# Weight tiles of another pitch and other fills beside two attentions, in a one-layer hybrid trunk

## The chip, the cores and the metric

The kernel runs on one core of a Trainium2 chip. The metric is the time of one execution in microseconds (us) on the device. A profiled execution has a time of its own, and its span, from the first to the last instruction, is a little shorter. Line numbers (L140) are those of the kernel before.

## The reference, cut to what matters

One residual layer over 1024 tokens of width 1024, all in float32:

```python
h = rmsnorm(x, norm1_g);  u = h @ w_in            # columns: mixers A, B, C, D and four gates
y_a = b_gate * conv3(c_gate * xa)                 # A: short gated convolution
y_b = stick_breaking_attention(q_b, k_b, v_b)     # B: 4 heads of 64
y_c = mamba2_mixer(u_c, ...)                      # C: conv4 + silu, dt = softplus, chunked scan, z gate
y_d = moba_attention(q_d, k_d, v_d)               # D: softmax attention over key blocks
merged = sum(sigmoid(u_g[i]) * (y_i @ w_branch[i]) for i in range(4))
x = x + merged @ w_o
g, up = split(rmsnorm(x, norm2_g) @ w_gate_up);  x = x + (silu(g) * up) @ w_down
return rmsnorm(x, final_g)
```

Both convolutions are causal: at the left edge they see zeros.

## The kernel before, in words

Every float32 matrix product is made of three matmuls (`mm3`, L137 to 142): each operand is split into a high part and a rest (`split`, L144: ScalarE writes the high part, VectorE subtracts), and high x high, high x rest and rest x high are added up in PSUM. A matmul has a stationary operand of 128 x 128 (the weights, loaded by LDWEIGHTS, "PEld" in the profile) and streams a moving operand of 512 columns.

SBUF tiles come from one pool with tags. Tag "w" has 8 buffers, each 1040 columns of four bytes wide, 4160 bytes a partition (`tw`, `PW`), of which nearly all tiles use 1024 columns. Tag "b" has 14 buffers of 4096 bytes, "t" has 6 of 8192. A tile waits for the release of the buffer that it takes over. The two sizes above 1024 columns are the weights of z and dt (`wz`, two tiles of 4 x 260 columns) and the inputs of the convolutions, which keep three (`craw`) or two (`cx`) columns of zeros at the left edge, set by GpSimd (L486, L624), and read shifted ranges behind them.

The stages follow each other:

- Head: x is normed, transposed and split into hT (`h0h`, `h0l`, `h1h`, `h1l`), eight token tiles in turn; `z_dt` (L243) makes z and dt of each tile, in an order written out by hand (`in_order`).
- `ssd` (L480): mixer C, with convolution, and beside it the projections of the first attention and `short_conv(0)`.
- Four attentions (`attend`, L386): two of softmax (mixer D), two of stick-breaking (mixer B, `stick_rows`: two sigmoids on ScalarE, a scan and a product on VectorE). Each goes through 8 units (2 heads x 4 query blocks of 256) with 1, 2, 3 and 4 steps, 20 steps in all. A step transposes two blocks of weights (`trp`, L403), splits them (`pt`) and multiplies the `pt` of the step before with v (`o`, L413).
- Beside an attention runs other work: `Fill` (L196) holds a list of generators and is called twice a step; `per_step` is how many turns of a generator a step brings. One turn is one `mm3` of 512 columns. `block` (L289) loads one weight tile and takes 16 turns; `qkv` and `short_conv` have three blocks each, 48 turns; `projected` has 32. `take` has no turns: it loads a branch's y and its projection weights (`w_branch`) and splits them. `fill.finish()` at an attention's end runs what is left.
- Branch products of A and B (`pr`, L823 on), with the sums of hT that the next stage needs (`sums_of_h`, on GpSimd and VectorE).
- Gates (`combine`, L766): 16 groups, each with seven products `prod` of 12 matmuls, from four token blocks by a scheme with sums (`four`). w[1], w[2] (operand `h0`), w[6] (`t2`) and w[7] (`t3`) are split into "w" tiles, w[5], w[3] (`h1`) and w[4] (`t4`) into "b" tiles.
- Output projection (moving operands in "w"), second norm and early products (`early`), FFN up (22 groups like the gates; `g` in place of `h`; the first 12 have two products less), and the last product (`product`, L1079), whose operands are in turn two "w" pairs (`hi`, `lo`) and three "t" pairs (`dhl`) of five.

The order on each engine is made once, before the run, from the whole program: mostly as written, with work drawn forward where an engine would stand idle.

The lines that order the fills are these:

```python
fill.gens += [qkv(B0, 1, sts[3])]
attend(sts[2], 0, stick_rows, 1, 2.4)
fill.gens += [take(2, c_), projected(2, c_), take(3, d_), short_conv(1, nc.gpsimd), projected(3, d_)]
attend(sts[3], 1, stick_rows, 1, 4.6)
```

Of the kernel before, what the change touches and what calls it, by code (L numbers as in the profile page):

```python
# [31 lines left out]
F32 = mybir.dt.float32  # L32
F32R = mybir.dt.float32r
# [6 lines left out]
P = 128  # L40
# [6 lines left out]
NEG = -1e30  # L47
PW = 1040
A0, B0, X0, D0 = 0, 6, 12, 16
# [3 lines left out]
def tile_hybrid_trunk(  # L53
# [31 lines left out]

    def tw(name, dt=F32):
        return mn.tile([P, PW], dt, tag="w", name=name, bufs=NB["w"])

    def big(name, tag="b", dt=F32):
        if tag == "w":  # L90
            return tw(name, dt)[:, :1024]
        return mn.tile([P, 1024], dt, tag=tag, name=name, bufs=NB[tag])
# [36 lines left out]

    def load_w(src, n=1024):  # L130
        raw = tw("wraw")
        nc.sync.dma_start(raw[:, :n], src)
        hi, lo = tw("whi", F32R), tw("wlo", F32R)
        split(hi[:, :n], lo[:, :n], raw[:, :n])
        return hi, lo
# [8 lines left out]
    def split(hi, lo, v):  # L144
        nc.scalar.copy(hi, v)  # L145
        nc.vector.tensor_sub(lo, v, hi.bitcast(F32))  # L146
# [49 lines left out]
    class Fill:  # L196
# [14 lines left out]

        def finish(self):
            self(1e9)

# [6 lines left out]
    dt = cp.tile([P, 8, 4], F32, name="dt")  # L221
    g1 = tw("g_sb")[:, :D]
    c2 = halves(big("c2a")) + halves(big("c2b"))
# [19 lines left out]
    def z_dt(t):  # L243
        o = psum("mm", "mmz")[:, :260]
        h = hT[t // 4]
        tl = slice((t % 4) * P, (t % 4 + 1) * P)
        for k in range(NK):
            if k == 4:
                yield
            w = wz[k // 4]  # L250
            c = slice((k % 4) * 260, (k % 4 + 1) * 260)
            mm3(o, (h[0][:, k, tl], h[1][:, k, tl]), (w[0][:, c], w[1][:, c]), k == 0, k == NK - 1)
        sg = c2[t % 4]
        nc.scalar.activation(sg[:, :256], o[:, :256], AF.Sigmoid)
        nc.vector.tensor_mul(sg[:, 256:], o[:, :256], sg[:, :256])
        nc.vector.tensor_add(dt[:, t, :], o[:, 256:260], dtb)
        nc.sync.dma_start(zdr[:, t, :], sg[:, 256:])

    load_x(0)
    nc.scalar.dma_start(g1, norm1_g.partition_broadcast(P))  # L260
    load_x(1)
    with in_order():
        norm1_stat(0)
        norm1_scale(0)
        norm1_stat(1)
        wz = [load_w(wzdt[0], 1040)]
        load_x(2)
        norm1_turn(0)
        norm1_scale(1)
        norm1_stat(2)  # L270
        wz.append(load_w(wzdt[1], 1040))
        for t in range(3, 8):
# [112 lines left out]

    def attend(st, p, rows, br, per_step):  # L386
        vv = st[3]
# [30 lines left out]
        for n, (j, cc) in enumerate(units):  # L418
# [18 lines left out]
            nc.gpsimd.dma_start(ydr[br][r, p, cc * 256:(cc + 1) * 256], yo[r])  # L437
        fill.finish()

# [40 lines left out]
    def ssd(per_chunk):  # L480
# [3 lines left out]
        for m in range(4):  # L484
            raw = tw("craw")
            nc.gpsimd.memset(raw[:, 0:3], 0.0)  # L486

            def put(half, t, o):
                nc.scalar.copy(raw[:, 3 + t.start:3 + t.stop], o)

            for _ in block(X0 + m, put):
                pass
            if m == 0:
                steps()
            acc = s8[0][:, m] if m < 2 else fm[:, m - 2]
            nc.vector.tensor_scalar(acc, raw[:, 3:3 + S], wc[:, m, 3:4], bc[:, m:m + 1],
                                    op0=ALU.mult, op1=ALU.add)
            for j in range(3):
                nc.vector.scalar_tensor_tensor(acc, raw[:, j:j + S], wc[:, m, j:j + 1], acc,
                                               op0=ALU.mult, op1=ALU.add)  # L500
            nc.scalar.activation(raw[:, :S], acc, AF.Sigmoid)
            nc.vector.tensor_mul(acc, acc, raw[:, :S])
            if m < 3:
# [118 lines left out]
    def short_conv(m, q=nc.sync):  # L622
        xa, cx = tw("xa"), tw("cx")
        nc.gpsimd.memset(cx[:, 0:2], 0.0)  # L624

        def put_x(_, t, o):
            nc.scalar.copy(xa[:, t], o)

        def put_c(_, t, o):
            nc.vector.tensor_mul(cx[:, 2 + t.start:2 + t.stop], o, xa[:, t])  # L630
            nc.vector.tensor_scalar_mul(xa[:, t], cx[:, 2 + t.start:2 + t.stop], wa[:, m, 2:3])
            for j in range(2):
                nc.vector.scalar_tensor_tensor(xa[:, t], cx[:, j + t.start:j + t.stop], wa[:, m, j:j + 1],
                                               xa[:, t], op0=ALU.mult, op1=ALU.add)

        def put_b(_, t, o):
            nc.vector.tensor_mul(xa[:, t], o, xa[:, t])

        yield from block(A0 + m, put_x)
        yield from block(A0 + 4 + m, put_c)  # L640
        yield from block(A0 + 2 + m, put_b)
        q.dma_start(ydr[0][:, m, :], xa[:, :S])

# [14 lines left out]
    def take(i, got):  # L658

        y = [[big(v, dt=F32R) for v in ("yhi", "ylo")] for _ in range(2)]  # L660
        w = [t8([2, 1024], "wbr") for _ in range(2)]
        w = [[v[:, 0], v[:, 1]] for v in w]
        for k in range(2):
# [28 lines left out]
    s8[0] = t8([2, S], "s8", F32)  # L692
    fill.gens += [qkv(B0, 1, sts[3])]
    attend(sts[2], 0, stick_rows, 1, 2.4)
    c_, d_ = [], []
    fill.gens += [take(2, c_), projected(2, c_), take(3, d_), short_conv(1, nc.gpsimd), projected(3, d_)]
    attend(sts[3], 1, stick_rows, 1, 4.6)
    pps.close()
# [546 lines left out]
```

## Time and profile before

| | |
|---|---|
| time, median of 3 runs | 1629.99 us (1629.48 to 1630.47) |
| the profiled execution | 1629.49 us, span 1627.8 us |
| TensorE matmuls (PE) | 1574.7 us busy, 7385 of them |
| weight loads (PEld) | 1285.0 us busy |
| VectorE (DVE) | 1175.8 us busy |
| ScalarE (ACT) | 660.5 us busy |
| GpSimd (POOL) | 187.5 us busy |

Busy times of different engines overlap. Matmuls are pipelined, and the end of each is modelled: a row of 0.39 us can be followed by the next one 0.23 us after its start, so the distance from start to start is what a matmul costs in a run of them. The granted clock (PEclk) is the share of TensorE's full clock that the chip granted.

### The profile page before, as it was taken

What the parts mean: (1) busy time and instruction counts of PE and PEld (TensorE: products, weight loads), DVE (VectorE), ACT (ScalarE), POOL (GpSimd) and SP (SyncE); (2) the same over time, 40 slices, a digit from 0 to 9 for tenths busy, and PEclk for the clock granted to TensorE, in tenths of its full rate; (3) what the DMA queues carried; (4) which work ended last, traced back from release to release, by engine and by line L of the source; (5) the groups of instructions that cost most, each with busy time, mean ns of one, the idle gap of its engine ahead of it and who ended that gap; (6) DMA issues with size and microseconds to landing.
All of it is one profiled execution on the core that took longest, in us unless ns stands there. A gap on an engine that the chain in (4) does not pass through costs nothing.

```text
span 1627.8 us, 20199 instructions
## 1 busy us (share of the span) xinstructions
PE 1574.7 (97%) x7385; PEld 1285.0 (79%) x7385; DVE 1175.8 (72%) x1725; ACT 660.5 (41%) x1072; POOL 187.5 (12%) x311
## 2 busy tenths in 40 slices
PE   6999999988999899999999999899999999999997
PEld 6888778776888688888887887688778888888885
DVE  5575687787674878777876547689999877656566
ACT  5343356565645633333333435321223322354343
POOL 1011020211205200000000011011001000010310
PEclk9999999999999999999999999999999999999999
DMA  4221211112316624343347545456764334897612
GB/s 172 69 93 63 74 35 35 42 40 70 135 53 214 241 85 155 111 147 104 130 129 257 208 149 180 157 216 231 262 241 187 149 149 149 309 407 255 189 49 104
DMA packets 88036, 245.97 MB, mean 151 GB/s; under 512 B 10400, under 2 KB 15552, under 8 KB 87936
## 3 DMA queue, kind: packets, MB, share of 16 engines
q1 hardware_dynamic: 69792, 181.49, 32.9%
q0 software_dynamic: 17712, 61.61, 9.5%
q10 hardware_dynamic: 432, 1.57, 0.3%
q8 instruction: 58, 0.95, 0.2%
q14 instruction: 42, 0.34, 0.1%
HBM read 172.00 MB, written 72.63 MB: 150 GB/s over the span
## 4 chain that ended last, share of the span: by engine, by line
PE 82%; DVE 10%; ACT 3%; issue 2%; DMA 2%; POOL 0%; SPq 0%; DVEq 0%; ACTq 0%; POOLq 0%
PE acc L156 13%; PE pp L140 12%; PE pp L142 12%; PE pp L141 12%; PE mm L140 4%; PE mm L142 4%; PE mm L141 4%; PE pp L156 4%; PE o L413 3%; PE acc L141 2%; PE acc L142 2%; PE trp L403 2%; PE acc L140 2%; DVE s L383 1%; DVE lo L146 1%
## 5 line engine op out<-in xcount | busy, mean ns | idle before, releaser
L145 ACT CAST hi<-s 128x1024 fp32r<-128x1024 f32 x76 | 77.2, 1049 | 179.8 <-DVE s L718 166.4
L156 PE MATMUL acc<-dhl 128*128 128x512 f32 x540 | 125.6, 390 | 0.0
L156 PEld LDWEIGHTS acc<-dhl 128*128 128x128 f32 x540 | 101.4, 188 | 21.3
L146 DVE TENSOR_TENSOR lo<-raw,hi 128x1024 fp32r<-128x1024 f32 x62 | 78.0, 1266 | 39.5 <-ACT hi L145 39.5
L146 DVE TENSOR_TENSOR lo<-s,hi 128x1024 fp32r<-128x1024 f32 x76 | 90.4, 1223 | 11.7 <-ACT hi L145 11.7
L785 ACT ACTIVATE g<-g 128x512 f32<-128x512 f32 x38 | 24.1, 633 | 154.2 <-DVE g L784 126.9
L145 ACT CAST hi<-raw 128x1024 fp32r<-128x1024 f32 x62 | 64.8, 1049 | 41.3 <-DMA raw<-in_wgu_dram 18.8
L146 DVE TENSOR_TENSOR dhl<-dr,dhl 128x1024 fp32r<-128x1024 f32 x45 | 58.4, 1311 | 30.7 <-ACT dhl L156 27.6
L146 DVE TENSOR_TENSOR pt<-trp,pt 128x512 fp32r<-128x512 f32 x80 | 54.5, 685 | 27.7 <-ACT pt L145 26.8
L140 PE MATMUL mm<-h0h,whi 128*128 128x512 f32 x176 | 73.0, 415 | 0.0
L140 PE MATMUL mm<-h1h,whi 128*128 128x512 f32 x176 | 72.9, 414 | 0.0
L156 ACT CAST dhl<-dr 128x1024 fp32r<-128x1024 f32 x45 | 47.1, 1052 | 58.5 <-PE acc L156 24.5
L141 PE MATMUL mm<-h0l,whi 128*128 128x512 f32 x176 | 70.3, 399 | 0.0
L142 PE MATMUL mm<-h0h,wlo 128*128 128x512 f32 x176 | 70.1, 398 | 0.0
L142 PE MATMUL mm<-h1h,wlo 128*128 128x512 f32 x176 | 70.0, 397 | 0.0
L141 PE MATMUL mm<-h1l,whi 128*128 128x512 f32 x176 | 69.9, 397 | 0.0
L413 PE MATMUL o<-pt,vv 128*128 128x256 f32 x320 | 60.6, 292 | 8.3 <-DVE pt L146 7.8
L142 PE MATMUL pp<-g1h,lo 128*128 128x512 f32 x176 | 68.6, 390 | 0.0
L140 PE MATMUL pp<-g1h,hi 128*128 128x512 f32 x176 | 68.5, 389 | 0.0
L141 PE MATMUL pp<-g1l,hi 128*128 128x512 f32 x176 | 68.5, 389 | 0.0
L413 PEld LDWEIGHTS o<-pt,vv 128*128 128x128 f32 x320 | 50.1, 190 | 22.6 <-DVE pt L146 12.7
L145 ACT CAST pt<-trp 128x512 fp32r<-128x512 f32 x80 | 47.2, 598 | 46.6 <-PE trp L403 43.7
(380 smaller groups left out, 4553.6 us busy)
## 6 DMA issues: line engine op xcount, KB each, us to landing
raw<-in_wgu_dram SPq DMA_DIRECT2D x56, 512.0 KB, 4.4
dr<-ffd SPq DMA_DIRECT2D x77, 256.0 KB, 4.5
raw<-in_wgate_dram SPq DMA_DIRECT2D x32, 512.0 KB, 5.3
raw<-prd SPq DMA_DIRECT2D x32, 512.0 KB, 4.2
wraw<-in_wmix_dram SPq DMA_DIRECT2D x22, 512.0 KB, 3.6
raw<-in_wd_dram SPq DMA_DIRECT2D x22, 512.0 KB, 4.3
wdd<-fs POOLq DMA_DIRECT2D x22, 512.0 KB, 3.5
ffd<-fs POOLq DMA_DIRECT2D x22, 512.0 KB, 4.0
```

The source lines that it names most:

```text
L140: nc.tensor.matmul(o, ah, bh, start=start, stop=False)
L141: nc.tensor.matmul(o, ah, bl, start=False, stop=False)
L142: nc.tensor.matmul(o, al, bh, start=False, stop=stop)
L145: nc.scalar.copy(hi, v)
L146: nc.vector.tensor_sub(lo, v, hi.bitcast(F32))
L156: setattr(e, n, lambda *a, _f=f, **k: tc.keep_in_program_order(_f(*a, **k)))
L383: nc.vector.tensor_tensor_scan(r, r, r, 1.0, ALU.mult, ALU.bypass)
L403: nc.tensor.transpose(tr[:, s * 256 + e * P:s * 256 + (e + 1) * P], pq[e][:, (s0 + s) * P:(s0 + s + 1) * P], identf)
L413: nc.tensor.matmul(o, vv[:, s0 + s, j, :], pt[:, i, s * 256:(s + 1) * 256], start=s0 + s + i == 0, stop=s0 + s + i == ns)
L785: nc.scalar.activation(g0[:, 512:], g0[:, 512:], act)
```

## The change

- Every "w" tile is 1024 columns, 4096 bytes; there are still 8. `g_sb`, the gain of the first norm, moves to a "b" tile.
- The weights of z and dt, 8 x 260 columns, are loaded into three tiles of 780, 780 and 520 columns, four loads in place of two, with the raw values in "w" and the two parts in "b" (`load_z`).
- The convolutions keep no zeros: the first term covers all columns and each shifted term only the columns that it reaches. The memsets go.
- The second short convolution stands behind the projections of the fourth attention, beside the third; the third has 3.6 turns a step instead of 2.4 and leaves one generator unfinished (`finish(left=1)`); the fourth has the rest of the convolution and both projections at 3.4 turns instead of 4.6.
- The weights of the second projection (`take(3)`) are split into "w" tiles instead of "t" tiles.

```diff
-PW = 1040
-    def tw(name, dt=F32):
-        return mn.tile([P, PW], dt, tag="w", name=name, bufs=NB["w"])
     def big(name, tag="b", dt=F32):
-        if tag == "w":
-            return tw(name, dt)[:, :1024]
         return mn.tile([P, 1024], dt, tag=tag, name=name, bufs=NB[tag])
...
-        def finish(self):
-            self(1e9)
+        def finish(self, left=0):
+            while len(self.gens) > left:
+                if next(self.gens[0], "end") == "end":
+                    self.gens.pop(0)
...
-    g1 = tw("g_sb")[:, :D]
+    g1 = big("g_sb")
...
-            w = wz[k // 4]
-            c = slice((k % 4) * 260, (k % 4 + 1) * 260)
+            w = wz[k // 3]
+            c = slice((k % 3) * 260, (k % 3 + 1) * 260)
...
+    def load_z(*src):
+
+        raw, hi, lo = big("zraw", "w"), big("zhi", dt=F32R), big("zlo", dt=F32R)
+        n = 0
+        for v in src:
+            nc.sync.dma_start(raw[:, n:n + v.shape[-1]], v)
+            n += v.shape[-1]
+        split(hi[:, :n], lo[:, :n], raw[:, :n])
+        return hi, lo
...
-        wz = [load_w(wzdt[0], 1040)]
+        wz = [load_z(wzdt[0][:, :780])]
...
-        wz.append(load_w(wzdt[1], 1040))
+        wz.append(load_z(wzdt[0][:, 780:], wzdt[1][:, :520]))
+        wz.append(load_z(wzdt[1][:, 520:]))
...
-        fill.finish()
+        fill.finish(left)
...
-            raw = tw("craw")
-            nc.gpsimd.memset(raw[:, 0:3], 0.0)
+            raw = big("craw", "w")
 
             def put(half, t, o):
-                nc.scalar.copy(raw[:, 3 + t.start:3 + t.stop], o)
+                nc.scalar.copy(raw[:, t], o)
...
-            nc.vector.tensor_scalar(acc, raw[:, 3:3 + S], wc[:, m, 3:4], bc[:, m:m + 1],
-                                    op0=ALU.mult, op1=ALU.add)
+            nc.vector.tensor_scalar(acc, raw, wc[:, m, 3:4], bc[:, m:m + 1], op0=ALU.mult, op1=ALU.add)
             for j in range(3):
-                nc.vector.scalar_tensor_tensor(acc, raw[:, j:j + S], wc[:, m, j:j + 1], acc,
+                nc.vector.scalar_tensor_tensor(acc[:, 3 - j:], raw[:, :S - 3 + j], wc[:, m, j:j + 1], acc[:, 3 - j:],
                                                op0=ALU.mult, op1=ALU.add)
...
-        xa, cx = tw("xa"), tw("cx")
-        nc.gpsimd.memset(cx[:, 0:2], 0.0)
+        xa, cx = big("xa", "w"), big("cx", "w")
...
-        w = [t8([2, 1024], "wbr") for _ in range(2)]
-        w = [[v[:, 0], v[:, 1]] for v in w]
+        if i == 2:
+            w = [t8([2, 1024], "wbr") for _ in range(2)]
+            w = [[v[:, 0], v[:, 1]] for v in w]
+        else:
+            w = [[big(v, "w", F32R) for v in ("whi", "wlo")] for _ in range(2)]
...
-    fill.gens += [qkv(B0, 1, sts[3])]
-    attend(sts[2], 0, stick_rows, 1, 2.4)
+    fill.gens += [qkv(B0, 1, sts[3]), short_conv(1, nc.gpsimd)]
+    attend(sts[2], 0, stick_rows, 1, 3.6, 1)
     c_, d_ = [], []
-    fill.gens += [take(2, c_), projected(2, c_), take(3, d_), short_conv(1, nc.gpsimd), projected(3, d_)]
-    attend(sts[3], 1, stick_rows, 1, 4.6)
+    fill.gens += [take(2, c_), projected(2, c_), take(3, d_), projected(3, d_)]
+    attend(sts[3], 1, stick_rows, 1, 3.4)
```

The convolution inside `short_conv` is changed in the same way as the one in `ssd`.

## Rows read from the trace of the kernel before

**Rows 1.** The page, busy time of the engines, share of the span, instructions

```profile
PE 1574.7 (97%) x7385; PEld 1285.0 (79%) x7385; DVE 1175.8 (72%) x1725; ACT 660.5 (41%) x1072; POOL 187.5 (12%) x311
```

**Rows 2.** Busy time by stretch: third and fourth attention, branch products, gates, FFN

```profile
321.00:396.00 75.00, 67.70 (x386) 53.55 (x384) 58.16 (x74) 43.49 (x92) 13.48 (x26) 1.00 0.18 57
396.00:508.00 112.00, 109.01 (x556) 89.32 (x555) 71.23 (x85) 64.28 (x124) 22.75 (x47) 0.98 0.35 121
508.00:560.00 52.00, 46.43 (x199) 37.16 (x198) 44.51 (x48) 31.15 (x53) 25.35 (x27) 0.99 0.56 206
560.00:869.00 309.00, 309.00 (x1342) 252.88 (x1341) 235.54 (x287) 103.41 (x132) 1.60 (x3) 1.00 0.38 131
...
1025.00:1410.00 385.00, 378.21 (x1631) 307.11 (x1630) 317.77 (x430) 102.97 (x135) 35.75 (x67) 0.99 0.56 199
```

**Rows 3.** Matmuls in order of time, first rows of products in two gate groups

```profile
598.92 0.40 PE L140 MATMUL pp<-h0h,hi 128*128 128x512 f32 x1
...
607.27 0.39 PE L140 MATMUL pp<-t3h,hi 128*128 128x512 f32 x1
...
609.99 0.39 PE L140 MATMUL pp<-h1h,hi 128*128 128x512 f32 x1
...
612.71 0.39 PE L140 MATMUL pp<-t4h,a 128*128 128x512 f32 x1
...
626.53 0.39 PE L140 MATMUL pp<-t3h,hi 128*128 128x512 f32 x1
...
629.32 0.39 PE L140 MATMUL pp<-h1h,hi 128*128 128x512 f32 x1
...
637.48 0.40 PE L140 MATMUL pp<-h0h,hi 128*128 128x512 f32 x1
```

**Rows 4.** Groups by line: count, busy us, mean ns, idle before

```profile
L140 PE MATMUL mm<-h0h,whi 128*128 128x512 f32 x176 | 73.0, 415 | 0.0
...
L140 PE MATMUL pp<-t2h,hi 128*128 128x512 f32 x152 | 61.2, 403 | 4.2 <-ACT hi L145 4.1
...
L140 PE MATMUL pp<-h0h,hi 128*128 128x512 f32 x128 | 51.4, 402 | 3.9 <-ACT pr L835 3.9
...
L156 PE MATMUL pp<-g0h,hi 128*128 128x512 f32 x96 | 38.5, 402 | 0.0
...
L140 PE MATMUL pp<-g0h,hi 128*128 128x512 f32 x80 | 31.6, 396 | 0.0
```

**Rows 5.** Matmuls of the last product, first row of two runs

```profile
1446.14 0.39 PE L156 MATMUL acc<-hi 128*128 128x512 f32 x1
...
1451.69 0.39 PE L156 MATMUL acc<-dhl 128*128 128x512 f32 x1
```

**Rows 6.** Waits of TensorE, 321 to 396 us, then 405.8 to 508: us, times, longest

```profile
PE o L413 <- DVE pt L146: 6.9, 6, 1.8
...
PE o L413 <- DVE pt L146: 0.3, 1, 0.3
```

**Rows 7.** Busy time by stretch at the fourth attention's start

```profile
397.00:402.40 5.40, 3.15 (x16) 1.73 (x14) 5.26 (x11) 4.61 (x10) 0.20 (x1) 1.00 0.48 155
402.40:405.80 3.40, 3.32 (x13) 3.13 (x14) 3.40 (x6) 2.23 (x6) 0.12 (x1) 0.51 0.00 0
```

**Rows 8.** Instructions in order of time in the head, SyncE's queue and TensorE

```profile
6.29 0.33 SPq L132 DMA_DIRECT2D wraw<-in_wzdt_dram  x1
...
14.12 1.07 PE L156 MATMUL trn<-identf,xn 128*128 128x128 f32 x8
16.24 0.38 PE L156 MATMUL mmz<-whi,h0h 128*128 128x260 f32 x1 [1.06 <-ACT whi L156]
...
20.00 1.90 PE L156 MATMUL trn<-identf,xn 128*128 128x128 f32 x8 [0.90 <-DVE ss L156]
```

**Rows 9.** A group by line, from 40 to 330 us

```profile
L486 POOL MEMSET craw<- 128x3 f32 x3 | 0.9, 304 | 23.1 <-DVE wlo L146 17.6 <-PE mmz L156 5.6
```

## The prediction before the change was run

> **What bounds the kernel now.** I read the page first, then the busy time by stage, then single matmuls in order of time, then the waits of TensorE. The page shows TensorE busy for 97% of the span and VectorE for 72% [rows 1]. So a gain can come only from TensorE's few idle places or from matmuls that follow each other faster. By stage, TensorE stands idle for 7.3 us of the third attention (75.0 less 67.7) and 3.0 us of the fourth (112.0 less 109.0), for 5.6 us of the two branch products after it, and for nothing in the gate stage [rows 2]. In the gate stage the distance from matmul to matmul is then the whole time.
>
> That distance has two sizes, which the group means hide. The product of w[7] with t3 has 12 matmuls. From its first row to the first row of the next product it takes 609.99 - 607.27 = 2.72 us in one gate group and 629.32 - 626.53 = 2.79 us in the next [rows 3]: 227 against 232 ns each. Line, operand t3 and shapes are the same, and TensorE waits for nothing. What differs is which of the eight "w" buffers holds the weights. 4160 is 4096 + 64, so the eight buffers start at eight different offsets from a multiple of 4096; "b" and "t" tiles have pitches of 4096 and 8192 and all start alike. I read the two sizes as a price of the start address of the weights, paid in most "w" tiles and in no other.
>
> **The change, part by part.** The sum is made against the profiled execution, 1629.5 us (span 1627.8).
>
> *Pitch 4096.* Two consecutive gate groups, 168 matmuls in 14 products, run from 598.92 to 637.48 [rows 3]: 38.56 us. At 2.72 a product they would take 38.08. So the 96 matmuls of the pair that take weights from "w" lose 0.48 us together, 5.0 ns each. Eight pairs: 3.8 us. The FFN takes "w" weights for t2 and t3 in all 22 groups (528 matmuls), for the first two products in ten groups (3 x 80) and in the early products (3 x 96) [rows 4]: 1056 x 5.0 ns = 5.3 us. In the last product 24 matmuls with both operands in "w" tiles take 1451.69 - 1446.14 = 5.55 us [rows 5], 231 ns. There are 384 of them, and 384 of the output projection that only stream from "w". At 4.6 ns each and three quarters of the buffers: 2.6 us. The 1056 matmuls of the input projection (six groups of 176) [rows 4] would give 5.3 us. They run beside attention, whose waits would take back some, so I count half, 2.6. The 192 branch products stand in a stage with VectorE busy 44.5 of 52 us [rows 2]; I count nothing. Together 14.3. Some of the FFN's saving goes into its own waits (TensorE idle 6.8 of 385 us there [rows 2]). I take **12.5 us**. Bounds: 9 (gates and FFN alone) and 15 (all counted).
>
> Here the Trainium skill speaks against the change. "TensorE: Matmul & The Clock Gate", section "Step-by-step: what each phase is for", says that the next weights come in through a read port of their own while a matmul streams, and that their load time goes by the number of columns; an address does not appear in it. By that rule this term is 0 and the sum below is -5.5. Rows 3 show one instruction at two speeds, which that rule leaves unexplained, so I follow the rows.
>
> *The fill rates.* One turn of the fill is three matmuls, 3 x 0.23 = 0.70 us. The third attention has 20 steps at 2.4 turns, 48 in all, exactly what its projection has: 1.7 us of cover a step. It is too little: TensorE waits 6.9 us in six places for pt, which VectorE splits after a scan [rows 6]. The fourth has 4.6 turns a step and waits 0.3 us after its start [rows 6]. At its start, with the fill used up, 5.4 us hold 3.15 us of TensorE work, and in the 3.4 us behind them the granted clock is 0.51, the lower of two levels, 1.2 GHz [rows 7]: 2.25 idle and 1.7 lost to the clock, 3.9 us.
>
> After the change the third attention has 72 turns: 48 of the projection and 24 of the short convolution. The other 24 are left, and the fourth has 68 paced turns of 24 + 64. So 20 turns, 14 us, run unpaced at the end, as before (92 of 112). The start of the fourth then always has turns ready: most of the 3.9 us goes, I count 3.5. The steady waits are 6.9 at 2.4 turns and 0.3 at 4.6; at 3.6 and 3.4 a straight line gives 3.3 and 3.9, no gain. A queue's waits fall faster than a line at first, so I take 2.0 and 2.2: 3.0 us gained. Together **6.5**. Bounds: 0 (straight line, and VectorE late at the start anyway) and 11 (all waits gone). VectorE pays for the moved 24 turns: one and a half blocks of weights split and half a convolution, some 6 us more in the third and less in the fourth. It was busy 58 of 75 us there and would be busy 64 of some 87; that fits, but little room is left.
>
> *Weights of z and dt.* Two loads of 1040 columns become four loads into tiles of 780, 780 and 520. The first z product then needs the second tile already at k = 3, and the next transposes stand behind it on TensorE in written order. Now the second load is issued at 6.29 us behind six of x, the transposes of the next token tile run at 14.12 and the second half of z waits until 16.24 [rows 8]. After: k = 3 stalls from 13.6 to about 16.3, the transposes follow it, and the two smaller splits cost one more fixed part on ScalarE and VectorE. The chain to the next row of transposes at 20.00 waits 0.9 us for its own scale [rows 8], which is the slack. I take **1.0 us lost**; bounds 0.5 gained (the first load is a quarter smaller) and 4 lost (two late splits and a spell at the lower clock, which at the fourth attention's start cost 1.7).
>
> *Convolutions.* The memsets of the left edge (0.3 us on GpSimd [rows 9]) go, and the shifted operations are one to three columns shorter. No product waits for those memsets: nothing either way; if one did, its 0.3 us.
>
> *Projection tiles.* The weights of the second projection stand in "w" rather than "t". Four of the eight "w" tiles are then held until its end. Branch 1's weights can use them only from there on, 20 us before they are needed at 531; the wait for the first gate weights, 3.9 us [rows 4], stays, since it follows VectorE's sums. Counted at nothing, hidden behind branch 0's products; the rival below prices it when that cover fails.
>
> Sum: -12.5 - 6.5 + 1.0 = -18.0, so 1611.5 us for the profiled execution, and with the median of before half a microsecond higher, **1612**.
>
> **The rivals.** *The fill only moves the waits.* VectorE is near its limit in the third attention, and what TensorE gains there it loses in the fourth at 3.4 turns. For it: the straight line above. Against: the start of the fourth is a gap that a left-over generator fills by construction. Time: 1629.5 - 12.5 + 1.0 + 0.5 = 1618.5.
>
> *The pitch does nothing.* The two speeds would come from something else that alternates with the groups, such as writes of the next weights. Against: the product behind the fast one takes its weights from "b" tiles, which are written in the same way, and needs 612.71 - 609.99 = 2.72 us [rows 3]. Time: 1630.0 - 6.5 + 1.0 = 1624.5. "SBUF — State Buffer", section on Door 1, gives lines of 16 bytes as the grain of full bandwidth; 4160 and 4096 are both multiples of 16, which agrees with this rival. No row here shows lines.
>
> *Slower: "w" tiles run out in the fourth attention.* The convolution holds two and its last block three; take(2) needs raw tiles, take(3) four more and raw tiles. If the loads and splits of both takes get their tiles only when the convolution is over and then queue one behind another, the projections are not ready. Each step without cover loses what VectorE is short of: its 58 us over 20 steps are 2.9 a step, against (67.7 - 48 x 0.70) / 20 = 1.7 of TensorE's own work [rows 2], so 1.2 us, and up to 1.6 with the latency. With 13 steps bare that is 21, plus 6 for a load and split in the open: 1612 + 27 = 1639. It decides when the first projection matmul comes later than the middle of the fourth attention; if only the second projection is late, half: about 1626 to 1628, no change. Against: the six tiles left beside the convolution suffice for a block's three and the raw tiles of a take, and 24 turns at 3.4 end a third of the way in.
>
> **How the numbers follow.** My forecast 66%, moved waits 14%, no pitch effect 8%, tiles short 7%, half short 5%. A measurement of this kernel tells about 0.2%, 3.3 us, from no change. The first three are faster by more than that: 88%; half short is the same, 5%; tiles short is slower, 7%. The bounds of the terms (9 to 15, 0 to 11, +0.5 to -4) put the likeliest case between 1604 and 1622; the range goes on to 1625 to take in the third case.
>
> **What would show it.** Right: every product of 12 matmuls at 2.72 us in the gate stage, and the last product's runs of 24 at 5.44; six waits for pt in the third attention shrunk to two or three; no spell at the lower clock near the fourth's start; first matmul of the input projection within 1 us of 47.8. Wrong: products at two speeds still; projection matmuls missing in the fourth attention's first half; the wait of 3.9 us at the gates longer. What would upset the sum most is another order of the instructions around the attentions, since the order is made anew from the whole program.

## The result, and the profile after the change

The changed kernel takes 1615.64 us (median; 1612.7 to 1616.85 in four runs) against 1629.74 us for the kernel before on the same chip (1627.42 to 1630.47). The ratio is 0.9913, with a 95% interval of 0.9896 to 0.993: 14 us faster. The forecast was 1612.0, its range 1604 to 1625. The profiled execution of the changed kernel took 1616.02 us, with a span of 1614.3. Line numbers below are those of the changed kernel: L134 to L136 are `mm3`, L139 and L140 `split`, L410 `trp`, L420 `o`; L150 stands for all of these in the parts whose order is written by hand. Runs whose edit adds lines have them two or three lines later.

Its page, busy time of the engines, answers to [rows 1]:

```profile
PE 1559.5 (97%) x7385; PEld 1281.2 (79%) x7385; DVE 1174.3 (73%) x1726; ACT 662.2 (41%) x1073; POOL 186.9 (12%) x305
```

TensorE does the same 7385 matmuls in 15.2 us less, and VectorE's work is unchanged. Where the time went is read from the first matmul of each stage in the two traces:

| stage, from its first matmul | before, at us | after, at us | length, after less before |
|---|---|---|---|
| head | 0 | 0 | -2.2 |
| mixer C, with projections (`mm`) | 47.7 | 45.5 | -1.4 |
| attentions 1 and 2 | 190.1 | 186.5 | +0.2 |
| attentions 3 and 4 (`z` with `m_s`) | 321.2 | 317.8 | -0.3 |
| branch products (`pr`) | 508.3 | 504.6 | 0.0 |
| gates (`pp`) | 558.7 | 555.0 | -3.0 |
| output projection, norm (`acc`) | 868.8 | 862.1 | -1.2 |
| early products (`pp<-g0`) | 962.0 | 954.1 | -0.9 |
| FFN up | 1041.7 | 1032.9 | -3.2 |
| last product (`acc<-dhl`), end | 1410.6 | 1398.6 | -1.5 |
| span | 1627.8 | 1614.3 | -13.5 |

The lengths are differences of the rounded starts, so each can be 0.1 off. 9.8 us came from the stages behind the branch products, whose code differs only in the pitch, 2.2 from the head, and almost nothing from the two attentions whose fills were remade.

*The gates.* Matmuls in order of time, the first rows of products in two consecutive groups, answer to [rows 3]:

```profile
595.59 0.39 PE L134 MATMUL pp<-h0h,hi 128*128 128x512 f32 x1
...
603.75 0.39 PE L134 MATMUL pp<-t3h,hi 128*128 128x512 f32 x1
...
606.47 0.39 PE L134 MATMUL pp<-h1h,hi 128*128 128x512 f32 x1
...
609.18 0.39 PE L134 MATMUL pp<-t4h,a 128*128 128x512 f32 x1
...
622.78 0.39 PE L134 MATMUL pp<-t3h,hi 128*128 128x512 f32 x1
...
625.50 0.39 PE L134 MATMUL pp<-h1h,hi 128*128 128x512 f32 x1
...
633.66 0.39 PE L134 MATMUL pp<-h0h,hi 128*128 128x512 f32 x1
```

The product with t3 takes 2.72 us in both groups (603.75 to 606.47, 622.78 to 625.50), where it took 2.72 and 2.79 before. The pair takes 633.66 - 595.59 = 38.07 us instead of 38.56. There is one speed now.

*The last product*, the same view, answers to [rows 5]: its 24 matmuls with both operands in "w" take 5.44 us, 227 ns each, instead of 5.55.

```profile
1434.00 0.39 PE L150 MATMUL acc<-hi 128*128 128x512 f32 x1
...
1439.44 5.83 PE L150 MATMUL acc<-dhl 128*128 128x512 f32 x25
```

*The third and fourth attention.* Busy time by stretch (columns: stretch, its length, then busy time and count of PE, PEld, DVE, ACT and POOL, the granted clock, the DMA share and GB/s), answers to [rows 2, 7]. With 72 turns instead of 48 the third attention now lasts to about 411.

```profile
318.00:411.00 93.00, 86.79 (x474) 69.63 (x474) 63.51 (x83) 48.36 (x103) 11.79 (x28) 1.00 0.10 29
411.00:505.00 94.00, 88.12 (x464) 71.27 (x463) 64.07 (x75) 59.60 (x114) 22.68 (x44) 1.00 0.47 163
```

TensorE stands idle for 93.0 - 86.8 = 6.2 us of the third and 94.0 - 88.1 = 5.9 us of the fourth, 12.1 together, and the granted clock is 1.00 throughout. Before, it stood idle for 7.3 and 3.0 us [rows 2], and the clock at the fourth's start cost 1.7 more [rows 7]: 12.0. Of that, 6.9 us were waits for pt in the third, 0.3 late in the fourth [rows 6], and 2.25 the hole at the fourth's start. The waits after the change, from the rows in order of time of the same kernel (in brackets the idle time before a row and what ended it):

```profile
341.96 0.61 PE L420 MATMUL o<-pt,vv 128*128 128x256 f32 x3 [1.49 <-DVE pt L140]
...
385.91 0.66 PE L410 MATMUL trp<-identf,pq 128*128 128x128 f32 x4 [1.78 <-DVE pt L140]
...
420.18 0.62 PE L420 MATMUL o<-pt,vv 128*128 128x256 f32 x3 [1.16 <-DVE pt L140]
431.12 0.62 PE L420 MATMUL o<-pt,vv 128*128 128x256 f32 x3 [1.23 <-DVE pt L140]
...
471.66 0.50 PE L420 MATMUL o<-pt,vv 128*128 128x256 f32 x2 [1.66 <-DVE pt L140]
```

Five waits for pt stand in the third attention (5.6 us, two of them shown) and four in the fourth (5.2 us, three shown): the end of the hole at the fourth's start was paid for by four waits behind it. VectorE is busy for only 68% of either stage, but without a break ahead of the waits. Busy time by stretch, before the waits at 341.96 and 385.91 (before the three of the fourth it is busy for 3.87 of 4.0, 4.00 of 4.0 and 3.57 of 3.6 us):

```profile
336.00:342.00 6.00, 4.51 (x25) 3.44 (x23) 5.87 (x5) 4.42 (x9) 0.00 (x0) 1.00 0.04 11
382.00:386.00 4.00, 2.22 (x13) 1.46 (x12) 3.97 (x4) 1.56 (x4) 0.00 (x0) 1.00 0.39 127
```

*The head*, SyncE's queue and TensorE in order of time, answers to [rows 8]:

```profile
2.70 1.61 SPq L260 DMA_DIRECT2D zraw<-in_wzdt_dram  x3
6.19 4.02 SPq L224 DMA_DIRECT2D xt<-in_x_dram  x5
...
14.96 0.39 PE L150 MATMUL mmz<-zlo,h0h 128*128 128x260 f32 x1 [0.67 <-DVE zlo L150]
...
15.31 1.03 PE L150 MATMUL trn<-identf,xn 128*128 128x128 f32 x8
19.19 1.06 PE L150 MATMUL trn<-identf,xn 128*128 128x128 f32 x8 [1.42 <-DVE ss L150]
```

All loads of z weights now stand ahead of x3 to x7, as the source of both kernels writes them. The wait in the first z product is 0.67 us where two of 1.06 and 0.89 stood, and the third row of transposes begins at 19.19 instead of 20.00. The spell at 1.2 GHz that followed there before (a granted clock of 0.50 over 20.1 to 23.5 us) is gone (1.00).

The head's length also goes by when the clock first rises, and that differs from run to run. A trace's record of the clock begins with its first rise: at 13.9 us after the change and 13.0 in pad64 (an experiment below), but at 19.1 in padmn256 and 19.5 in pad128, whose heads are made from the same code. The input projection begins at 45.5 in the first two and at 46.4 and 46.5 in the others. So 2.2 us is the head's gain with an early rise, and 1.2 with a late one.

### The profile page after: what moved, and what is told of

Its sections match the earlier page's. It is cut to its first block, busy times and chain, and to the rows that moved or that the text cites. A ratio compares the mean times of both kernels' runs of the same rounds, so it can differ in the third digit from the quotient of the medians.

```text
span 1614.3 us, 20185 instructions
## 1 busy us (share of the span) xinstructions
PE 1559.5 (97%) x7385; PEld 1281.2 (79%) x7385; DVE 1174.3 (73%) x1726; ACT 662.2 (41%) x1073; POOL 186.9 (12%) x305
## 4 chain that ended last, share of the span: by engine, by line
PE 81%; DVE 12%; issue 3%; ACT 2%; DMA 2%; POOL 0%; SPq 0%; DVEq 0%; ACTq 0%
PE acc L150 13%; PE pp L134 12%; PE pp L136 12%; PE pp L135 12%; PE mm L134 4%; PE mm L136 4%; PE pp L150 4%; PE mm L135 4%; PE o L420 2%; DVE s L390 2%; PE acc L135 2%; PE acc L136 2%; PE acc L134 2%; PE trp L410 2%; DVE lo L140 1%
## 5 line engine op out<-in xcount | busy, mean ns | idle before, releaser
L139 ACT CAST hi<-s 128x1024 fp32r<-128x1024 f32 x76 | 77.3, 1052 | 180.5 <-DVE s L726 174.3
L150 PE MATMUL acc<-dhl 128*128 128x512 f32 x540 | 125.3, 389 | 0.0
L150 PEld LDWEIGHTS acc<-dhl 128*128 128x128 f32 x540 | 101.3, 188 | 21.0
L140 DVE TENSOR_TENSOR lo<-raw,hi 128x1024 fp32r<-128x1024 f32 x62 | 77.6, 1259 | 42.1 <-ACT hi L139 42.1
L140 DVE TENSOR_TENSOR lo<-s,hi 128x1024 fp32r<-128x1024 f32 x76 | 90.4, 1222 | 11.8 <-ACT hi L139 11.8
L139 ACT CAST hi<-raw 128x1024 fp32r<-128x1024 f32 x62 | 64.9, 1051 | 41.3 <-DMA raw<-in_wgu_dram 17.8
L140 DVE TENSOR_TENSOR dhl<-dr,dhl 128x1024 fp32r<-128x1024 f32 x45 | 58.5, 1313 | 30.3 <-ACT dhl L150 28.8
L134 PE MATMUL mm<-h0h,whi 128*128 128x512 f32 x176 | 72.8, 414 | 0.0
L134 PE MATMUL mm<-h1h,whi 128*128 128x512 f32 x176 | 72.4, 411 | 0.1
L140 DVE TENSOR_TENSOR pt<-trp,pt 128x512 fp32r<-128x512 f32 x80 | 54.6, 685 | 24.5 <-ACT pt L139 24.1
L150 ACT CAST dhl<-dr 128x1024 fp32r<-128x1024 f32 x45 | 47.3, 1057 | 57.3 <-PE acc L150 22.4
L136 PE MATMUL mm<-h1h,wlo 128*128 128x512 f32 x176 | 70.1, 398 | 0.0
L136 PE MATMUL mm<-h0h,wlo 128*128 128x512 f32 x176 | 69.8, 396 | 0.0
L134 PE MATMUL pp<-g1h,hi 128*128 128x512 f32 x176 | 68.5, 389 | 0.0
L136 PE MATMUL pp<-g1h,lo 128*128 128x512 f32 x176 | 68.5, 389 | 0.0
L420 PE MATMUL o<-pt,vv 128*128 128x256 f32 x320 | 59.2, 289 | 9.5 <-DVE pt L140 9.3
L139 ACT CAST pt<-trp 128x512 fp32r<-128x512 f32 x80 | 47.6, 599 | 49.0 <-PE trp L410 44.3
L420 PEld LDWEIGHTS o<-pt,vv 128*128 128x128 f32 x320 | 49.7, 189 | 20.8 <-DVE pt L140 12.8
```

Source lines behind the costliest of these rows:

```text
L134: nc.tensor.matmul(o, ah, bh, start=start, stop=False)
L136: nc.tensor.matmul(o, al, bh, start=False, stop=stop)
L150: setattr(e, n, lambda *a, _f=f, **k: tc.keep_in_program_order(_f(*a, **k)))
L420: nc.tensor.matmul(o, vv[:, s0 + s, j, :], pt[:, i, s * 256:(s + 1) * 256], start=s0 + s + i == 0, stop=s0 + s + i == ns)
```

## The theories

On the pitch there were two. *Start address*, the prediction's: a "w" tile whose address is off makes its matmuls slow. *Distance*: what counts is how far two tiles are apart, and alike offsets cost nothing. The second has two forms: the distance between the two operands that TensorE reads, or between what it reads and what other engines write at that time. For the distance spoke a count over the trace of before: sorted by the addresses of the built program, the 512-column matmuls behind 560 us stand 227 ns apart (mean start to start, 2642 of them) where the weights of a matmul and of the next lie a multiple of 256 bytes from the moving operand, and 233, 233 and 232 ns (503, 261 and 245) where both lie 64, 128 or 192 bytes beside one.

On the fills: *gain*, the prediction's 6.5 us from fewer waits, against *moved waits*, its first rival.

All ratios below are to the kernel before on the same chip (medians 1628.7, 1628.4 and 1629.4 us in the three sets).

## The experiments

**pad64 and pad128: all large tiles moved together.** An unused constant of 64 (or 128) bytes a partition ahead of every large tile:

```diff
+    pad = cp.tile([P, 16], F32, name="pad")      # pad128: [P, 32]
+    nc.gpsimd.memset(pad, 0.0)
```

> The changed kernel with 64 bytes of unused constants in front of all large tiles: every tile of every tag starts 64 bytes later, the pitches stay at multiples of 4096. Theory 'start address': weights that do not start at a multiple of 256 bytes make each matmul of 512 columns 5 to 6 ns longer, now in all tiles, about 5,000 matmuls behind 505 us: 25 to 30 us slower than the changed kernel, 1641 to 1646 us, all gate products near 2.79 us. Rival 'distance': what costs is the odd distance between the tile that is read and the tiles that are written meanwhile; the distances are unchanged, so 1616 us and products of 2.72 us.

> The same with 128 bytes. Theory 'start address' with a grain of 256 bytes: as with 64 bytes, 1641 to 1646 us. The same theory with a grain of 128 bytes: 1616 us. Rival 'distance': 1616 us.

Measured: 1615.21 us (1615.1 to 1615.86), ratio 0.9918 [0.9902, 0.9933], and 1614.6 us, ratio 0.991 [0.9897, 0.9924]. Nothing changed, although every large tile begins 64 or 128 bytes beside its old place. Matmuls in order of time of pad64, two consecutive gate groups, still take 632.92 - 594.84 = 38.08 us:

```profile
594.84 0.39 PE L136 MATMUL pp<-h0h,hi 128*128 128x512 f32 x1
...
632.92 0.39 PE L136 MATMUL pp<-h0h,hi 128*128 128x512 f32 x1
```

The start address falls.

**pitch4160: the change with the old pitch.**

```diff
-        return mn.tile([P, 1024], dt, tag=tag, name=name, bufs=NB[tag])
+        n = 1040 if tag == "w" else 1024
+        return mn.tile([P, n], dt, tag=tag, name=name, bufs=NB[tag])[:, :1024]
```

> The changed kernel with the pitch of the w tiles alone put back to 4160 bytes; fills, loads and convolutions as changed. If the pitch made the gain as predicted: 12.5 us slower than the changed kernel, 1628 us; by the difference of the two traces per stage, 9.7 behind 505 us and 1.2 in the first two attentions and the scan, 11 us, 1627. Rival 'the gain came from the order of the work': 1616 us.

Measured: 1627.31 us (1626.51 to 1628.74), ratio 0.9991 [0.9982, 1.0]. On the same chip pad64, which has the pitch of 4096, took 12.1 us less. The pitch is nearly all of the gain; fills, head and convolutions together give 1.4 us at this pitch.

**fill_back: the change with the old fills**, pitch 4096, the old "t" tiles for the second projection, the new loads of z:

```diff
-    fill.gens += [qkv(B0, 1, sts[3]), short_conv(1, nc.gpsimd)]
-    attend(sts[2], 0, stick_rows, 1, 3.6, 1)
+    fill.gens += [qkv(B0, 1, sts[3])]
+    attend(sts[2], 0, stick_rows, 1, 2.4)
     c_, d_ = [], []
-    fill.gens += [take(2, c_), projected(2, c_), take(3, d_), projected(3, d_)]
-    attend(sts[3], 1, stick_rows, 1, 3.4)
+    fill.gens += [take(2, c_), projected(2, c_), take(3, d_), short_conv(1, nc.gpsimd), projected(3, d_)]
+    attend(sts[3], 1, stick_rows, 1, 4.6)
```

> The changed kernel with the fills of the third and fourth attention and the weight tiles of the second projection put back as before; the pitch stays at 4096. Predicted worth of the new fills: 6.5 us, 1622 us. By the two traces the third and fourth attention together are 0.3 us shorter only: 1616 us, with waits of about 7 us for pt in the third attention, nearly none in the fourth, and the spell at the lower clock at the fourth's start back.

Measured: 1618.08 us (1616.36 to 1620.36), ratio 0.9935 [0.9922, 0.9947]: 2.9 us more than pad64, between the two times that had been named. With the old fills the hole at the fourth's start is back, with a longer spell at 1.2 GHz than before, and another one in the third. Busy time by stretch of fill_back (the clock is the third column from the end):

```profile
377.00:380.40 3.40, 3.40 (x13) 2.94 (x14) 3.34 (x5) 0.59 (x1) 1.47 (x3) 0.57 0.02 5
398.00:404.80 6.80, 6.08 (x22) 4.66 (x23) 6.30 (x8) 4.94 (x9) 0.21 (x1) 0.50 0.00 1
```

(1 - 0.57) x 3.4 + 0.50 x 6.8 = 4.9 us go to the clock, and TensorE's idle time over both attentions is 11.2 us, no more than the 12.1 after the change. The stage from the third attention to the branch products is 190.8 us long, 4.0 more than after the change; part of that is given back in the gates, where this run has no spell at the lower clock. The fills are thus worth some 3 us here, and at the old pitch 1.4 together with the head, against 6.5 in the prediction; and what they save is the lower clock, not idle time.

**padmn64 and padmn256: one pool moved against another.** The constant now stands between the pool of h and g (`h0`, `h1`, `g0`, `g1`) and the pool of "w", "b" and "t":

```diff
+    pd = ctx.enter_context(tc.tile_pool(name="pd", bufs=1))
     mn = ctx.enter_context(tc.tile_pool(name="mn", bufs=2, reuse_waits="tile"))
...
+    pad = pd.tile([P, 16], F32, name="pad")      # padmn256: [P, 64]
+    nc.gpsimd.memset(pad, 0.0)
```

> The changed kernel with 64 unused bytes between the pool of h0, h1, g0, g1 and the pool of all other large tiles. All tiles with tags w, b and t keep their distances among each other and are 64 bytes further from the h and g tiles. Theory 'two streams of TensorE': a matmul is long when its moving operand and the weights loaded around it start at addresses whose distance is not a multiple of 256 bytes. Then the products with h0, h1, g0 and g1 are long (four of seven in a gate group, three of five or five of seven in the FFN, all early products), those with t2, t3 and t4, the output projection's and the last product's are not: 1824 x 6 ns = 11 us behind the branch products and 1 or 2 in the input projection, 1627 us. Rival 'reads against the writes of other engines': split and load targets keep their distance from the weights that are read, so 1615 us and 2.72 us for every product.

> The same unused constant at the same place as the 64 bytes between the pool of h and g and the pool of w, b and t, but 256 bytes long. If only the distance modulo 256 bytes counts, the products of h and g are at 2.72 us again and the time is 1615.6. If any distance that is not a multiple of 1024 or 4096 costs, it is 1628 as with 64 bytes.

Measured: 1629.1 us (1627.58 to 1631.04), ratio 1.0003 [0.9993, 1.0012], with 64 bytes, and 1614.98 us (1614.71 to 1616.74), ratio 0.9917 [0.9904, 0.9931], with 256. An unused constant of 64 bytes takes back the whole gain. Matmuls in order of time of padmn64 show where:

```profile
598.26 0.39 PE L137 MATMUL pp<-h0h,hi 128*128 128x512 f32 x1
...
606.60 0.39 PE L137 MATMUL pp<-t3h,hi 128*128 128x512 f32 x1
...
609.32 0.39 PE L137 MATMUL pp<-h1h,hi 128*128 128x512 f32 x1
...
612.12 0.39 PE L137 MATMUL pp<-t4h,a 128*128 128x512 f32 x1
...
637.05 0.39 PE L137 MATMUL pp<-h0h,hi 128*128 128x512 f32 x1
```

The product that streams t3, from the same pool as its weights, takes 2.72 us; the next one, which streams h1 from the moved pool, 2.80. Weights, other engines' work and order are those of the other runs. The pair takes 38.79 us, in padmn256 again 38.08:

```profile
594.93 0.39 PE L137 MATMUL pp<-h0h,hi 128*128 128x512 f32 x1
...
633.01 0.39 PE L137 MATMUL pp<-h0h,hi 128*128 128x512 f32 x1
```

The last product, which takes nothing from h or g, is unmoved in padmn64 (215.7 us from its first matmul to the end, as after the change). So it is the distance between the weights and the moving operand that counts, and 256 bytes are as good as 0. Whether it is a matmul's own weights, or those that are loaded for the next one while it streams, these runs don't tell apart: within a product both lie at the same distance.

Other engines write into "w", "b" and "t" tiles meanwhile, and in padmn64 these too lie 64 bytes off h, so the rows above alone do not rule their writes out. The count over padmn64's trace does: behind 560 us, where no instruction of VectorE, ScalarE or GpSimd writes to SBUF during the step, it takes 233.3 ns at a distance of 64 (215 steps) and 226.6 at 0 (238); where one does, 233.4 and 227.4. Writes by DMA were not sorted out.

The distance is not the whole rule. In the last product of the kernel before, seven runs of 12 matmuls have both operands 64 bytes beside a multiple of 256, so at a distance of 0, and still stand 230 ns apart; two rows of before, in order of time, bound one of them (2.76 us):

```profile
1487.25 0.39 PE L156 MATMUL acc<-hi 128*128 128x512 f32 x1
...
1490.01 0.39 PE L156 MATMUL acc<-hi 128*128 128x512 f32 x1
```

They follow matmuls whose operands lie at multiples of 256. Their first ten steps take 231 ns, the last two 226. So a change of offset from one run to the next seems to cost something too; that was not tested.

**r40_40, r46_34, r34_46, r50_34 and r46_30: other rates.** Only the two rates differ, turns a step in the third and in the fourth attention (3.6 and 3.4 in the change). For r46_34:

```diff
-    attend(sts[2], 0, stick_rows, 1, 3.6, 1)
+    attend(sts[2], 0, stick_rows, 1, 4.6, 1)
```

> The changed kernel with 4.0 turns a step in both stick-breaking attentions instead of 3.6 and 3.4, so that all 160 turns are paced and none is left for the end. If the steady waits go by the rate (6 us at 3.4 to 3.6 in each, 0.3 at 4.6), each has some 3 us: 6 us faster than the changed kernel, 1610 us. Rival 'the unpaced 20 turns at the end covered what the branch products wait for': the saving comes back as a gap ahead of the branch products, 1615 us.

> 4.6 turns a step in the third attention, 3.4 in the fourth: 92 turns, then 68, none left. The third's waits go to some 0.5 us and the fourth's stay near 6: 6 us faster, 1610 us. Rival 'VectorE sets the third attention' (it has the convolution's products too): its waits stay, 1615 us.

> 3.4 turns a step in the third, 4.6 in the fourth: 68, then 92, none left. The fourth's waits go to some 0.5 us, the third's stay near 6: 6 us faster, 1610 us. With the run before it this tells which of the two attentions needs the cover.

> The fill at 5.0 turns a step in the third attention (100 turns, 28 more than the projection and the first half of the convolution need) and 3.4 in the fourth. If the third's waits for pt were all that 4.6 took away, nothing is left to gain there and turns are missing at the fourth's start: 1613.5 to 1616. If cover in the third goes on paying: 1611.

> 4.6 turns a step in the third attention as in the best run so far, and 3.0 instead of 3.4 in the fourth. If the fourth's waits at 3.4 were from too little cover a step, they grow: 1615 or more. If they come from taking too many turns too early, as at 4.6, they shrink: 1611.

| third, fourth | us, median | ratio [95%] |
|---|---|---|
| 4.0, 4.0 | 1616.76 (1615.44 to 1618.41) | 0.9926 [0.9914, 0.9939] |
| 4.6, 3.4 | 1613.51 (1612.72 to 1614.3) | 0.9906 [0.9892, 0.9919] |
| 3.4, 4.6 | 1623.32 (1621.69 to 1624.08) | 0.9964 [0.9951, 0.9976] |
| 5.0, 3.4 | 1617.03 (1615.82 to 1618.08) | 0.9927 [0.9913, 0.994] |
| 4.6, 3.0 | 1612.47 (1612.21 to 1613.82) | 0.9901 [0.9888, 0.9915] |

At 4.6 the third attention's waits for pt are gone (0.4 us in r46_34 and r46_30), but of the 6 us that had been expected for it some 2 came: the fourth took the rest. Busy time by stretch of r46_30, whose third attention lasts to 419; TensorE is idle for 1.1 us of the third and 7.5 of the fourth:

```profile
318.00:419.00 101.00, 99.88 (x533) 80.94 (x533) 69.67 (x91) 50.80 (x105) 11.80 (x27) 1.00 0.17 53
419.00:502.00 83.00, 75.55 (x401) 60.49 (x401) 58.05 (x67) 56.71 (x110) 22.32 (x44) 0.98 0.42 150
...
430.00:433.40 3.40, 3.40 (x12) 2.42 (x11) 3.40 (x4) 2.52 (x6) 0.78 (x2) 0.52 0.39 157
```

The hole at the fourth's start is back, with a spell at 1.2 GHz from 430 to 433.4. The sum, 1.1 + 7.5 + 0.48 x 3.4 = 10.2, is 2 us under the change's 12.1. On one chip r46_30 took 1612.47 us and padmn256, which is the change but for its unused constant, 1614.98, with no overlap of their runs; of the 2.2 us between their two profiles 1.5 lie in these two attentions and 0.9 in the head, where the clock rose at 13.7 us in one and at 19.1 in the other. This is the best version found. Neither 4.0 and 4.0 nor 5.0 and 3.4 did better than the change: the first keeps 3.8 and 4.3 us of waits for pt and has one spell of 3.4 us at 1.2 GHz in the fourth, the second waits 0.5 and 4.7 us for pt and has two.

The opposite, 3.4 and 4.6, is 8 us slower than the change. Its waits, third attention and fourth, from the rows in order of time:

```profile
384.56 0.66 PE L410 MATMUL trp<-identf,pq 128*128 128x128 f32 x4 [1.53 <-DVE pt L140]
...
421.00 0.50 PE L136 MATMUL mm<-h0h,wlo 128*128 128x512 f32 x1 [1.09 <-DVE wlo L140]
...
476.59 0.39 PE L420 MATMUL o<-pt,vv 128*128 128x256 f32 x1 [1.85 <-ACT pt L139]
477.52 1.04 PE L134 MATMUL pc<-yhi,whi 128*128 128x512 f32 x2 [0.55 <-ACT yhi L139]
```

The third keeps its waits, and the fourth, asked for 4.6 turns a step, runs into the splits of the turns' own operands (wlo, yhi) and a spell of 6.8 us at a granted clock of 0.52 from 478 on. So more turns a step did not mean fewer waits in the fourth.

**head_x: the loads of z in the order that the prediction assumed**, behind x3 to x5:

```diff
+        for t in range(3, 6):
+            load_x(t)
         wz.append(load_z(wzdt[0][:, 780:], wzdt[1][:, :520]))
         wz.append(load_z(wzdt[1][:, 520:]))
-        for t in range(3, 8):
+        for t in range(6, 8):
             load_x(t)
```

> The order that the prediction assumed for the head: x2 to x5 are issued ahead of the second and third load of the z weights, as in the kernel before. By the prediction's own step the first z product then stalls at its fourth k, and the first matmul of the input projection comes 1.0 us later than before's 47.7, about 48.7, against 45.5 in the changed kernel; the run ends some 3 us later, about 1618.5. Rival: the two smaller loads land early enough behind x2 to x5 as well, and the start at 45.5 came from the smaller tiles alone: no change, 1615.6.

Measured: the first matmul of the input projection comes at 48.2 us, against 45.5 after the change and 47.7 before. SyncE's queue and TensorE in order of time of head_x:

```profile
2.18 2.46 SPq L224 DMA_DIRECT2D xt<-in_x_dram  x4
6.16 1.52 SPq L260 DMA_DIRECT2D zraw<-in_wzdt_dram  x3
...
15.67 0.58 PE L150 MATMUL mmz<-zhi,h0h 128*128 128x260 f32 x1 [1.85 <-ACT zhi L150]
16.67 0.58 PE L150 MATMUL mmz<-zlo,h0h 128*128 128x260 f32 x1 [0.42 <-DVE zlo L150]
```

The stall at the fourth k is there: 1.85 + 0.42 us. The time of the whole run, 1616.86 us (1615.82 to 1619.77), ratio 0.9928 [0.9916, 0.9941], lies 1.9 us over padmn256 on the same chip; the ranges overlap. In the traces the input projection begins 1.8 us later than in padmn256 (46.4) and 2.7 later than after the change. But the clock rose only at 21.4 us in head_x, later than in any other run (12.7 to 19.5), and how much of the delay is the clock and how much the stall itself can't be told from one trace.

## Why the prediction was right, and where not

**The pitch, -12.5.** The size was right: -12.1 (pitch4160 against pad64), -11.0 by the stages of the profile (-9.8 behind the branch products, -1.2 in mixer C and the first attentions). The gate pair came out at 38.07 us where 38.08 was forecast. Term by term: the gates 3.0 instead of 3.8 (part of the saving went to a spell at the lower clock, 6.8 us long instead of 3.4; pad64 and padmn256, which differ in it, gave 3.2 and 3.8); FFN and early products 4.1 instead of 5.3; output projection and last product 2.7 instead of 2.6; input projection 1.2 instead of 2.6; branch products 0, as forecast. The input projection's 512-column matmuls stand 229.7 ns apart after the change and 231.0 before (means over the pairs of neighbours behind 50 us), so beside the attentions most of their lateness has another source, which was not sought. The upper bound of 15 is not the sum of all terms: with the whole input projection they come to 17.0.

What failed is the sentence "I read the two sizes as a price of the start address of the weights". It is the distance between weights and moving operand. The sum did not suffer, because in the gates, the FFN and the input projection the moving operands of before all lay at multiples of 256 bytes from the "b" and "t" tiles (8 x 4160 = 33280 = 130 x 256), so that a start address that is off and a distance that is off were the same buffers. In the output projection it is the moving operand that was off and the weights were not; by its own sentence the prediction should have counted nothing there, and it counted them. That the sum came out so near is thus in part luck: with h 64 bytes further, as in padmn64, tiles of pitch 4096 gain nothing (1629.1 us).

The Trainium skill, "TensorE: Matmul & The Clock Gate", section "Step-by-step: what each phase is for", gives the weights a read port of their own and names no address, by which the term is 0. That does not agree with the runs: 64 bytes between two pools are worth 14 us. Nor do the 16-byte lines of the Trainium skill's page "SBUF — State Buffer", section on Door 1, mark the grain here: 64 is a multiple of 16 and costs. The rival "the pitch does nothing" (1624.5) falls by the 12.1 us of pitch4160.

**The fills, -6.5.** This term failed, and the first rival, moved waits, had the mechanism. The step that failed is "A queue's waits fall faster than a line at first, so I take 2.0 and 2.2". At 3.6 and 3.4 turns the waits for pt are 5.6 and 5.2 us, more than the straight line's 3.3 and 3.9. The waits come where VectorE is busy without a break for 4 to 6 us, and up to 3.6 turns a step do not cover that; 4.6 do in the third. The 3.9 us at the fourth's start went as forecast, and the lower clock with them, but the four waits behind took as much. Measured: -0.3 by the two profiles, 2.9 by fill_back. VectorE's load in the third was met: 63.5 of 93 us, where 64 of 87 was forecast.

**z and dt, +1.0.** The sign was wrong: -2.2, or -1.2 with a late rise of the clock. The step was "issued behind six of x": the order was made anew, and all z loads went ahead of x3. With the old order head_x shows the forecast stall, and its input projection begins 0.5 us later than before's (48.2 less 47.7). So the stall was foreseen rightly and the assumption on the order was not; its price is not shown, since the clock rose at 13.2 us and fell once more in before, and rose at 21.4 in head_x. Why the order came out so was not tried.

**Convolutions and tiles, 0.** Kept: the wait ahead of the gates is 4.4 us where it was 3.9 (both traces put its end down to ScalarE's copy of `pr`, not to VectorE's sums as the prediction has it), and the first product of a projection comes at 438.8, 28 us into the fourth attention and so before the middle that was named as the point from which late tiles decide. The rival that ended slower did not come; in r34_46 something like it did, at 8 us.

Of the signs that the prediction named for being right, two came (gate products at 2.72 us and the last product's runs at 5.44, no spell at the lower clock near the fourth's start) and two did not (five waits for pt in place of two or three, the input projection at 45.5 in place of 47.8). The misses have opposite signs: -11.0 - 0.3 - 2.2 = -13.5 against -18.0 forecast, and the span lost 13.5. That 1612 lies so near is in part luck, since the head gave back half of what the fills did not bring.

## What to carry to other kernels

Where a matmul has two speeds in one trace and waits for nothing, compare the addresses of its two operands with each other, not each with a round number: in these kernels nothing was lost where the pitch of every tile that TensorE reads, and the gap between pools, was a multiple of 256 bytes. Before counting on a fill rate, look how long the other engine is busy without a break ahead of the waits; a mean rate that lies under that burst only moves the waits. And where an order is made anew from the whole program, a moved load is worth nothing on paper until the queue of the built program has been read.

## What the runs showed of the hardware that was not expected

A 512-column matmul stands 226.8 ns behind the one before it when its weights lie a multiple of 256 bytes from its moving operand (mean of 4430 behind 560 us after the change), and 233.3 ns when they lie 64 bytes beside one (1786 in padmn64). 64, 128 and 192 bytes cost about the same in the kernel before; smaller offsets were not tried, and why the chip does so stays open.

In the head, matmuls of 260 columns stand 0.22 us apart up to 21.1 us in head_x, but only up to 13.4 in the changed kernel, and 0.12 later on, though the profile's column for the granted clock reads 1.00 for both over 8 to 21 us. That column shows 1.00 where the trace has no record, and the record begins at 21.4 and 13.9 us, where the step changes. In the kernel before, a spell that is on record at 0.50 has the same step of 0.22 us. So TensorE ran at the lower clock up to there. Busy time by stretch and matmuls in order of time of before, then matmuls of head_x:

```profile
20.10:23.50 3.40, 3.40 (x17) 3.40 (x18) 1.97 (x5) 2.15 (x5) 0.45 (x1) 0.50 0.11 39
...
22.13 0.42 PE L156 MATMUL mmz<-whi,h0l 128*128 128x260 f32 x1
22.35 0.42 PE L156 MATMUL mmz<-whi,h0h 128*128 128x260 f32 x1
```

```profile
20.71 0.42 PE L150 MATMUL mmz<-zhi,h0l 128*128 128x260 f32 x1
20.93 0.42 PE L150 MATMUL mmz<-zhi,h0h 128*128 128x260 f32 x1
...
23.01 0.28 PE L150 MATMUL mmz<-zhi,h0l 128*128 128x260 f32 x1
23.13 0.28 PE L150 MATMUL mmz<-zhi,h0h 128*128 128x260 f32 x1
```
